# Two-layer hybrid backbone step: the last split weights of one token group used first for the other, the first modulation turned as one tile, grouped heads' scores in F32

## The chip, the cores and the metric

The kernel runs on one core of a Trainium2 chip. The metric is the device time of one execution in microseconds, as the median of several runs; less is better.

## The reference

One inference step of a two-layer backbone with model width 1024, for 128 context tokens and 512 latent tokens (640 in all). Each layer has a mixer and a SwiGLU FFN (hidden width 2816), each between an RMS norm with shift and scale before it and an RMS norm with a gate after it. Shift, scale and gate come from a small product, `silu(c) @ ada_w + ada_b`, one row for context and one for latent tokens. Layer 0 mixes with a short gated convolution and a conformer branch with a 31-tap depthwise convolution; layer 1 with grouped-query attention (8 heads of 64, 2 key heads) beside latent attention (8 heads); latent tokens read 640 keys, 128 cached and their own 512, context tokens their own 128. Cut to the parts that matter:

```python
hp = _modulate(_rmsnorm(xp, norm_pre[l, 0]), mp[:, 0], mp[:, 1])    # context; the same for latent (hs)
op = _conv_mixers(hp, *cargs)                                       # layer 0
q = _rmsnorm((h @ w_in)[..., :512].reshape(.., 8, 64), q_norm)      # layer 1, grouped heads
k = _rmsnorm((h @ w_in)[..., 512:640].reshape(.., 2, 64), k_norm)   # rotary on q and k of latent tokens
p = softmax(scale * q @ k.T); o = p @ v                             # context reads its 128 keys, latent 640: 128 cached and 512 own
xp = xp + mp[:, 2][:, None, :] * _rmsnorm(op, norm_post[l, 0])
fp = _modulate(_rmsnorm(xp, norm_pre[l, 1]), mp[:, 3], mp[:, 4])
xp = xp + mp[:, 5][:, None, :] * _rmsnorm(_swiglu(fp, w_gate, w_up, w_down), norm_post[l, 1])
```

All of it is in F32; the outputs are the tokens and the new key and value rows of the context.

## The kernel before

Activations lie with features on the 128 partitions and tokens along the free axis. A linear layer is split into two numbers of reduced precision (fp32r): `gran` (L123) loads a raw tile of 128x1024 weights through SP's queue, ACT casts it to `whi` (L134), VectorE (DVE) or GpSimd subtracts to give `wlo` (L139); `block` (L160) gives such pairs for some K tiles, and `mm3` (called by `lin`) issues three matmuls for each K tile, `whi` times the high half of x, `whi` times its low half, `wlo` times the high half (L175, L187, L189). `raw`, `whi` and `wlo` have four buffers each.

Tokens are worked on in groups: `GA` is columns 0 to 255, `GB` 256 to 639, `AB` both, `FULL` two of 320. A layer's stages overlap at their boundaries: where a mixer ends and the next stage begins, GA's boundary work (norms, gate, modulation) runs beside GB's products, and so GA goes first through the next stage's first blocks, then GB. In those places (`gu` and the last `down` of the FFN, `conv_in`'s first half, conv's and attention's output products, attention's input products) every weight block is loaded, cast and subtracted once for GA and once again for GB. Each boundary has statistics on PE (`st`), an inverse square root of twelve short DVE operations (`rvb`, `rgb`, `rhb`, then three rounds of `rtb`, `rtb`, `rzb`; L283 to L294), and `spread`, which hands the result to all partitions through PE. A scheduler puts the instructions of each engine in order at build time from its own estimates and from priorities; the engines then run in that fixed order.

The modulation: `ada0` at the start and, in the background of the convolution, `adaw` (a coroutine, `ada`, advanced by `spawn`) multiply c against `ada_w`, four column tiles of 2 rows (PE tile 128*2) into rows 0, 32, 64, 96 of one PSUM tile; `ada_out` copies four rows of two and turns them with sixteen tiny transposes (`adat`) into columns (`mods`). The depthwise convolution of the latent tokens is done on PE with 32*32 tiles (`tap`), 16 beside each other. The scores of a unit (one head, 128 queries) go into a PSUM tile `s` of two halves of 320 keys, of which there are two; then follow max, exponent, transposes (`pT`) on PE with copies to SBUF, and the value product (`av`) of two heads in column tiles of 64. The grouped heads' queries and keys are kept as high and low halves stacked on the partitions (`qS`, `kS`, `kL`, fp32r), the latent heads' as plain F32 (`qM`, `kM`).

The input projections of attention: for each group `attn_q` (products `pq`), `attn_kv` (`pkf`, `pvf`), `attn_k`, `attn_qa` (`pqa`, then `qa`), `attn_c` (`pcf`, `pkrf`), and `store_k`, `store_v`, `store_c`, which put keys, values and the compressed keys where attention reads them.

## Time and profile before

| | |
|---|---|
| median of three runs | 1697.18 us (1695.88 to 1697.71) |
| the profiled execution | 1697.65 us, span 1695.9 us |
| TensorE (PE) busy | 1632.8 us, 96% |
| weight loads of TensorE (PEld) | 1507.8 us, 89% |
| VectorE (DVE) | 968.0 us, 57% |
| ScalarE (ACT) | 655.1 us, 39% |
| GpSimd (POOL) | 217.3 us, 13% |
| read from memory | 190.99 MB, 116 GB/s over the span |

The table is from the profile's page of that execution. PE's share of the span does not say that it ran at its peak; the stages differ, which is why the profile is read by stage: start and first projection to 164 us, taps to 187, the rest of conv to 335, the FFN of layer 0 to 816, attention's projections to 945, attention to 1143, its output product to 1240, the FFN of layer 1 to the end. A row of the timeline gives start and length of merged instructions; because matmuls are pipelined, the time one of them costs is the distance from its start to the next start, not its length.

### The profile page before, as it was taken

How to read it: one execution, taken by the hardware profiler on the slowest of the kernel's cores; microseconds unless marked ns; L12 is line 12 of the kernel's file. 1: busy time of each engine (PE TensorE's matmuls, PEld its weight loads, DVE VectorE, ACT ScalarE, POOL GpSimd, SP SyncE). 2: the span in 40 equal slices, each digit the busy share in tenths (PEclk: the TensorE clock that was granted, in tenths of full speed). 3: DMA queues.
4: the chain of work that ended last, by engine and by line, in shares of the span. 5: the costliest groups of instructions: out<-in, count | busy, mean ns of one | idle time of the engine just before them, and what ended most of it. 6: DMA issues, size and time to landing. Idle time of an engine off the chain costs nothing.

```text
span 1695.9 us, 28690 instructions
## 1 busy us (share of the span) xinstructions
PE 1632.8 (96%) x11569; PEld 1507.8 (89%) x11569; DVE 968.0 (57%) x2021; ACT 655.1 (39%) x1222; POOL 217.3 (13%) x239
## 2 busy tenths in 40 slices
PE   6999999989999999999988899999999999999998
PEld 2577599989999999999988786769899999999998
DVE  3767055888784735837988655455888102111246
ACT  2321135653222211234555576665643222212234
POOL 2000000110000000001202121111102333333301
PEclk9999999999999999999999799999999999999999
DMA  9764014347463433525344010025354222222232
GB/s 339 233 222 148 30 50 130 113 129 226 143 200 112 137 100 98 157 88 174 104 136 100 8 38 14 1 80 173 119 174 151 78 85 75 75 76 75 75 108 104
DMA packets 174406, 198.37 MB, mean 117 GB/s; under 512 B 18788, under 2 KB 152881, under 8 KB 174273
## 3 DMA queue, kind: packets, MB, share of 16 engines
q1 hardware_dynamic: 172224, 194.94, 36.8%
q8 instruction: 90, 1.47, 0.4%
q10 hardware_dynamic: 1600, 1.49, 0.3%
q14 instruction: 44, 0.35, 0.1%
q0 software_dynamic: 448, 0.11, 0.0%
HBM read 190.99 MB, written 5.52 MB: 116 GB/s over the span
## 4 chain that ended last, share of the span: by engine, by line
PE 86%; DVE 8%; DMA 3%; issue 2%; ACT 1%; DVEq 0%; POOL 0%; SPq 0%; ACTq 0%; POOLq 0%
PE pd L175 6%; PE pd L187 6%; PE pd L189 6%; PE pu L175 6%; PE pu L189 6%; PE pu L187 6%; PE pg L189 5%; PE pg L175 5%; PE pg L187 5%; PE av L1408 3%; PE tap L787 2%; PE s L1355 2%; PE po L187 2%; PE po L175 2%; PE po L189 2%; PE pT L975 2%
## 5 line engine op out<-in xcount | busy, mean ns | idle before, releaser
L134 ACT CAST whi<-raw 128x1024 fp32r<-128x1024 f32 (+1 forms) x260 | 264.1, 1018 | 445.1 <-PE pd L187 112.1
L139 DVE TENSOR_TENSOR wlo<-raw,whi 128x1024 fp32r<-128x1024 f32 (+3 forms) x219 | 258.5, 1182 | 137.7 <-ACT whi L134 133.3
L175 PE MATMUL pd<-hid,whi 128*128 128x320 f32 (+2 forms) x704 | 181.5, 310 | 0.0
L189 PE MATMUL pd<-hid,wlo 128*128 128x320 f32 (+2 forms) x704 | 181.4, 309 | 0.0
L187 PE MATMUL pd<-hid,whi 128*128 128x320 f32 (+2 forms) x704 | 181.2, 309 | 0.0
L623 DVE TENSOR_TENSOR sg<-pu,sg 128x320 f32<-128x320 f32 (+2 forms) x88 | 39.9, 483 | 247.0 <-PE pu L189 247.0
L175 PE MATMUL pu<-h,whi 128*128 128x320 f32 (+2 forms) x704 | 177.0, 311 | 0.0
L187 PE MATMUL pu<-h,whi 128*128 128x320 f32 (+2 forms) x704 | 176.7, 310 | 0.0
L187 PE MATMUL pg<-h,whi 128*128 128x320 f32 (+2 forms) x704 | 176.6, 310 | 0.0
L189 PE MATMUL pg<-h,wlo 128*128 128x320 f32 (+2 forms) x704 | 176.2, 310 | 0.0
L189 PE MATMUL pu<-h,wlo 128*128 128x320 f32 (+2 forms) x704 | 176.1, 310 | 0.0
L175 PE MATMUL pg<-h,whi 128*128 128x320 f32 (+2 forms) x704 | 176.1, 310 | 0.0
L139 POOL TENSOR_TENSOR wlo<-raw,whi 128x1024 fp32r<-128x1024 f32 (+1 forms) x48 | 112.0, 2339 | 234.7 <-ACT whi L134 234.7
L385 DVE SCALAR_TENSOR_TENSOR acc<-adaw,cT,acc 128x512 f32<-128x512 f32 x168 | 123.9, 790 | 11.2 <-DMA adaw<-in_ada_w 11.0
L187 PEld LDWEIGHTS pd<-hid,whi 128*128 128x128 f32 x704 | 123.5, 188 | 0.0
L189 PEld LDWEIGHTS pd<-hid,wlo 128*128 128x128 f32 x704 | 123.5, 188 | 0.0
L175 PEld LDWEIGHTS pd<-hid,whi 128*128 128x128 f32 x704 | 123.4, 188 | 0.0
L187 PEld LDWEIGHTS pu<-h,whi 128*128 128x128 f32 x704 | 122.9, 189 | 0.0
L175 PEld LDWEIGHTS pu<-h,whi 128*128 128x128 f32 x704 | 122.8, 189 | 0.0
L189 PEld LDWEIGHTS pg<-h,wlo 128*128 128x128 f32 x704 | 122.7, 189 | 0.0
L187 PEld LDWEIGHTS pg<-h,whi 128*128 128x128 f32 x704 | 122.7, 189 | 0.0
L189 PEld LDWEIGHTS pu<-h,wlo 128*128 128x128 f32 x704 | 122.7, 189 | 0.0
(457 smaller groups left out, 3065.3 us busy)
## 6 DMA issues: line engine op xcount, KB each, us to landing
raw<-in_ffn_w_gate SPq DMA_DIRECT2D x56, 512.0 KB, 3.9
raw<-in_ffn_w_up SPq DMA_DIRECT2D x56, 512.0 KB, 3.7
raw<-in_ffn_w_down SPq DMA_DIRECT2D x56, 512.0 KB, 3.4
adaw<-in_ada_w SPq DMA_DIRECT2D x96, 256.0 KB, 3.0
raw<-in_ada_w SPq DMA_DIRECT2D x36, 512.0 KB, 4.1
raw<-in_conv_w_in SPq DMA_DIRECT2D x24, 512.0 KB, 4.5
raw<-in_attn_w_in SPq DMA_DIRECT2D x16, 512.0 KB, 4.1
raw<-in_attn_w_out SPq DMA_DIRECT2D x16, 512.0 KB, 3.5
```

The costliest lines, as they stand in the source:

```text
L134: nc.scalar.copy(hi[:, :kt, :cols], rv)
L139: (self.nc.vector if (le or next(self.lo_mix)) == "dve" else self.nc.gpsimd).tensor_tensor(o, x, h, ALU.subtract)
L175: ins = [mm(o, whi, h, start=first, stop=False) for o, (h, l) in zip(outs, xs)]
L187: mm(o, whi, l, start=False, stop=False)
L189: mm(o, wlo, h, start=False, stop=last)
L385: ins = nc.vector.scalar_tensor_tensor(acc[v], w, self.cT[:, v, k:k + 1], acc[v], ALU.mult, ALU.add)
L623: nc.vector.tensor_tensor(tv(sg[i]), uv, tv(sg[i]), ALU.mult)
L787: nc.tensor.matmul(ps[i][32 * j:32 * j + 32, :LAT], d[r, j], zs[j][r, at + t:at + t + LAT], start=(t == 0), stop=(t == CFK - 1))
L975: self.nc.tensor.transpose(ps, src, self.ident[:m, :m])
L1355: mm(o, qM[(h - 8) // 2][:96, h % 2, qs], kM[h - 8][:96, k0:k0 + n], start=True, stop=True)
L1408: nc.tensor.matmul(av[o:o + 64, :w], value(u.h, k), u.pt[:, 0] if qt == 0 else u.pt[:, :, i], start=(i == 0), stop=(i == len(ks) - 1))
```

## The change

Four edits. **Kept weights**: in each GA, GB pair the last blocks of GA (`gu` b = 2; `down`, conv out and attention out cb = 2, 3; both blocks of conv_in's first half; both of `attn_c`) are kept in their buffers and used first for GB, in the order 2, 3, 0, 1. **`ada_out`**: the PSUM tile is zeroed first, 98 rows are copied at once and turned with four transposes of 128x98, two additions of 16 columns follow; at the start this and the first modulation of GA have high priority. The coroutine `ada` starts at the first block of GB, before it started ahead of GA. **Scores of the grouped heads**: the query lies in F32 in `qF`, once plain and once with its halves exchanged, the keys in `kF` with keys 0 to 447 in rows 0 to 63 and 320 to 767 in rows 64 to 127 (from 448), and each half of the score block is one F32 matmul, from rows 0 to 63 and from rows 64 to 127 (a 64*128 tile). **Order of attention's projections**: `attn_c` of GB goes ahead of `attn_kv`, and the two `store_c` ahead of `attn_qa`.

```diff
+                nc.vector.memset(ps[:98], 0.0)
...
-        for j in range(4):
-            r = slice(32 * j, 32 * j + 2)
-            self.copy(engines[j], row[r], ps[r, :])
-        for j in range(4):
-            r = slice(32 * j, 32 * j + 2)
-            pt = alloc("adat")
-            for c in range(4):
-                self.nc.tensor.transpose(pt[:, 2 * c:2 * c + 2], row[r, c * P:(c + 1) * P], self.ident[r, r])
-            c0 = 4 * (ch + j)
-            for v in range(2):
-                self.nc.vector.tensor_tensor(self.mods[l][:, v, c0:c0 + 4], pt[:, :8].rearrange("p (c v) -> p v c", v=2)[:, v],
-                                             self.par["ada_b"][:, 48 * l + c0:48 * l + c0 + 4], ALU.add)
+        n = 512 // len(engines)
+        for i, e in enumerate(engines):
+            self.copy(e, row[:98, i * n:i * n + n], ps[:98, i * n:i * n + n])
+        pt = alloc("adat")
+        for c in range(4):
+            self.nc.tensor.transpose(pt[:, c * P:c * P + 98], row[:98, c * P:(c + 1) * P], self.ident[:98, :98])
+        o = pt.rearrange("p (c j r) -> p j c r", c=4, r=32)
+        c0 = 4 * ch
+        for v in (0, 1):
+            m, b = self.mods[l][:, v, c0:c0 + 16], self.par["ada_b"][:, 48 * l + c0:48 * l + c0 + 16]
+            q = lambda x: x.rearrange("p (j c) -> p j c", c=4)
+            self.nc.vector.tensor_tensor(q(m), o[:, :, :, v], q(b), ALU.add)
...
-        def gu(b, chunks):
-            g, u = self.block(wg, 0, KD, b * 256, 256), self.block(wu, 0, KD, b * 256, 256)
+        def gu(b, chunks, gu_=None):
+            g, u = gu_ or (self.block(wg, 0, KD, b * 256, 256), self.block(wu, 0, KD, b * 256, 256))
...
+        gu(2, ins[1], kept)
+        for b in range(2):
             gu(b, ins[1])
...
+                kept = {}
                 for ch in order:
-                    for cb in range(4):
-                        down(k0, kt, ch, cb, False)
+                    for cb in (range(4) if ch == order[0] else (2, 3, 0, 1)):
+                        w = down(k0, kt, ch, cb, False, kept.get(cb))
+                        if cb > 1:
+                            kept[cb] = w
...
+        with self.tc.high_priority(BOUND_PRIO):
+            self.ada_out(0, 0, ps, ("act", "dve"), self.pp)
+            for v in range(2):
+                nc.vector.scalar_tensor_tensor(a[:, v], m[:, v, KD:2 * KD], 1.0, self.par["norm_pre"][:, 0:KD], ALU.add, ALU.mult)
         H = [self.t5([P, 2, TOK], R32, name=f"h{k}") for k in range(KD)]
-        for v in range(2):
...
-        self.spawn(ada)
...
-            b2 = self.block(w, 0, KD, 3 * SCW + 512 + 256 * hb, 256)
-            b1 = self.block(w, 0, KD, 3 * SCW + 256 * hb, 256)
+            if (hb, chs) == (0, GB):
+                self.spawn(ada)
+            if chs != GB:
+                b2 = self.block(w, 0, KD, 3 * SCW + 512 + 256 * hb, 256)
+                b1 = self.block(w, 0, KD, 3 * SCW + 256 * hb, 256)
...
-                qS = st["qS"][t][:, hh, s:s + n]
-                nc.scalar.copy(qS[r], f[r])
-                nc.vector.tensor_tensor(qS[o], f[r], fl(qS[r]), ALU.subtract)
+                nc.scalar.copy(sw[o], f[r])
...
+    def keys_in(self, st, g, k0, x):
+
+        m = x.shape[1]
+        for a, b, r, c in ((k0, min(k0 + m, KH), 0, 0), (max(k0, KH), k0 + m, 64, KH - SEQ)):
+            if a < b:
+                self.copy(("act", "dve")[g], st["kF"][g][r:r + 64, a - c:b - c], x[:, a - k0:b - k0])
...
-            if ORD:
-                self.attn_c(H, GB, rb)
-                self.store_c(GA, st, ra)
-                self.store_c(GB, st, rb)
-                self.attn_qa(H, GB, st)
-            else:
-                self.attn_qa(H, GB, st)
-                self.store_c(GA, st, ra)
-                self.attn_c(H, GB, rb)
-                self.store_c(GB, st, rb)
+            self.store_c(GA, st, ra)
+            self.store_c(GB, st, rb)
+            self.attn_qa(H, GB, st)
...
-                    q, g = st["qS"][h // 2][:, h % 2, qs], h // 4
-                    mm(o, q, st["kS"][g][:, k0:k0 + n], start=True, stop=False)
-                    mm(o, q, st["kL"][g][:, k0:k0 + n], start=False, stop=True)
+                    r = slice(64 * c, 64 * c + 64)
+                    k0 = 0 if qt == 0 else SEQ
+                    mm(o, st["qF"][h // 2][r, (h + c) % 2, qs], st["kF"][h // 4][r, k0:k0 + n], start=True, stop=True)
```

What the new order looks like: names with numbers are buffers; `tap` is one tap of the convolution in one of sixteen tiles, `adaw` a matmul of the next modulation. On PE, in the last third of the taps, before (the rows of the second modulation are turned here):

```order
L787 MATMUL tap<-z_466,dg 32x512
L787 MATMUL tap<-z_467,dg 32x512
L470 MATMUL adat<-con,arow 128x2 x4
L787 MATMUL tap<-z_468,dg 32x512
L470 MATMUL adat<-con,arow 128x2 x4
L787 MATMUL tap<-z_465,dg 32x512
L787 MATMUL tap<-z_466,dg 32x512
```

and after, where the same modulation's matmuls now stand in three places among the taps, this one the second:

```order
L799 MATMUL tap<-z_445,dg 32x512
L456 MATMUL adaw<-raw,cM 2x512
L799 MATMUL tap<-z_446,dg 32x512
L799 MATMUL tap<-z_443,dg 32x512
L456 MATMUL adaw<-raw,cM 2x512
L799 MATMUL tap<-z_444,dg 32x512
L456 MATMUL adaw<-raw,cM 2x512
L799 MATMUL tap<-z_445,dg 32x512
L456 MATMUL adaw<-raw,cM 2x512
L799 MATMUL tap<-z_446,dg 32x512
L799 MATMUL tap<-z_443,dg 32x512
```

The turning left the taps and the products came into them. On PE at the end of attention's projections, where `pqa` is the last product, `rz` the inverse square roots that `spread` needs, `nc`, `stc` and `stqa` statistics and transposes of compressed keys and queries, before:

```order
L189 MATMUL pqa<-h_7893,wlo 128x384
L1352 MATMUL s<-kS_9087,qS_8345 128x128
L1353 MATMUL s<-kL_9089,qS_8345 128x128
L1352 MATMUL s<-kS_9087,qS_8345 128x128
L1353 MATMUL s<-kL_9089,qS_8345 128x128
L313 MATMUL spread<-con,rz 128x128 x2
L975 MATMUL nc<-con,cf0a 128x128
L975 MATMUL nc<-con,cf1a 128x128
L306 MATMUL stc<-con,csq 128x1 x3
L313 MATMUL spread<-con,rz 128x128 x3
L306 MATMUL stqa<-con,qsq 128x1 x3
L175 MATMUL mqr<-qa_8342,whi 128x320
```

and after:

```order
L190 MATMUL pqa<-h_7747,wlo 128x384
L1360 MATMUL s<-kF_8905,qF_8175 128x128 x2
L1360 MATMUL s<-kF_8905,qF_8175 128x320 x2
L997 MATMUL pT<-con,prob 128x128
L1360 MATMUL s<-kF_8905,qF_8175 128x320 x2
L997 MATMUL pT<-con,prob 128x128
L314 MATMUL spread<-con,rz 128x128 x2
L1360 MATMUL s<-kF_8905,qF_8175 128x320 x2
L997 MATMUL pT<-con,prob 128x128 x5
L997 MATMUL nc<-con,cf0a 128x128
L997 MATMUL nc<-con,cf1a 128x128
L307 MATMUL stc<-con,csq 128x1 x3
```

Four score blocks of head 0 and transposes of its first units now stand between the last product and the statistics. On DVE, in the boundary of the FFN before attention's projections, in the chain of twelve operations that ends in `rzb`, before (from its fourth operation):

```order
L291 TENSOR_TENSOR rtb<-rgb 128x3
L1044 TENSOR_TENSOR qS_8345<-qf,qS_8345 64x256 x2
L985 STREAM_SHUFFLE sw<-qf 128x128
L292 TENSOR_TENSOR rtb<-rtb,rhb 128x3
L139 TENSOR_TENSOR wlo<-raw,whi 128x1024
L987 TENSOR_TENSOR qf<-qf,rope 128x128
L294 SCALAR_TENSOR_TENSOR rzb<-rtb,rgb 128x3
L1044 TENSOR_TENSOR qS_8346<-qf,qS_8346 64x256
L1038 COPY ssq<-stq 128x2x2
L1044 TENSOR_TENSOR qS_8346<-qf,qS_8346 64x256
L139 TENSOR_TENSOR wlo<-raw,whi 128x1024
```

and after, from its first:

```order
L284 TENSOR_SCALAR rvb<-st 128x3
L286 TENSOR_SCALAR rgb<-rvb 128x3
L289 TENSOR_SCALAR rhb<-rvb 128x3
L292 TENSOR_TENSOR rtb<-rgb 128x3
L293 TENSOR_TENSOR rtb<-rtb,rhb 128x3
L295 SCALAR_TENSOR_TENSOR rzb<-rtb,rgb 128x3
L292 TENSOR_TENSOR rtb<-rzb 128x3
L293 TENSOR_TENSOR rtb<-rtb,rhb 128x3
L295 SCALAR_TENSOR_TENSOR rzb<-rtb,rzb 128x3
L292 TENSOR_TENSOR rtb<-rzb 128x3
L293 TENSOR_TENSOR rtb<-rtb,rhb 128x3
L295 SCALAR_TENSOR_TENSOR rzb<-rtb,rzb 128x3
```

The subtractions for the queries are gone, and neither weights nor rotary operations stand within the chain.

## Rows read from the trace of the kernel before

**Rows 1.** From the first part of the page: busy time, share of the span and instructions of each engine.
```profile
PE 1632.8 (96%) x11569; PEld 1507.8 (89%) x11569; DVE 968.0 (57%) x2021; ACT 655.1 (39%) x1222; POOL 217.3 (13%) x239
```

**Rows 2.** The table by stage: busy time of each engine in a stretch (with its instructions), TensorE's granted clock as a share of full speed, the share of the DMA engines and GB/s. The four stretches are the input projections of attention in three parts and the first part of attention.
```profile
816.50:868.70 52.20, 44.12 (x339) 42.76 (x337) 46.69 (x137) 26.53 (x48) 8.79 (x10) 0.93 0.50 150
868.70:926.60 57.90, 56.88 (x343) 54.45 (x344) 52.33 (x140) 29.49 (x67) 10.50 (x9) 1.00 0.34 83
926.60:945.00 18.40, 8.09 (x34) 7.14 (x33) 13.80 (x58) 7.39 (x17) 0.76 (x2) 0.58 0.25 57
945.00:1035.50 90.50, 88.27 (x611) 72.00 (x610) 55.09 (x105) 64.53 (x159) 18.91 (x43) 0.97 0.06 18
```

**Rows 3.** From the costliest groups on the page: line, engine, operation, output and inputs, count, then busy time and mean ns of one, then idle time before and who ended it.
```profile
L139 DVE TENSOR_TENSOR wlo<-raw,whi 128x1024 fp32r<-128x1024 f32 (+3 forms) x219 | 258.5, 1182 | 137.7 <-ACT whi L134 133.3
```

**Rows 4.** The waits of PE over the whole span: who waited for whom, us in total, times, longest.
```profile
PE st L519 <- DVE sq L516: 10.9, 6, 4.4
...
PE po L175 <- ACT z L268: 1.9, 1, 1.9
```

**Rows 5.** The timeline of PE in the depthwise convolution (taps), instructions of one kind in a row merged: start, us from first start to last end, line, operation, tile of the array (rows*columns), shape, count of records.
```profile
164.21 23.68 PE L787 MATMUL tap<-z,dg 32*32 32x512 f32 x724
187.82 1.02 PE L454 MATMUL adaw<-raw,cM 128*2 128x512 f32 x2
188.77 1.04 PE L787 MATMUL tap<-z,dg 32*32 32x512 f32 x2
189.74 1.02 PE L454 MATMUL adaw<-raw,cM 128*2 128x512 f32 x2
...
196.37 0.41 PE L470 MATMUL adat<-con,arow 2*128 2x2 f32 x4
```

**Rows 6.** From PE's groups by form: the scores of a latent head against one half of the keys.
```profile
L1355 PE MATMUL s<-kM,qM 96*128 96x320 f32 x128 | 41.5, 446 | 0.2 <-ACT prob L1383 0.2
```

**Rows 7.** The timeline of all engines at the start, around the first modulation.
```profile
33.84 1.03 PE L710 MATMUL ada<-ada0w,cM 128*2 128x512 f32 x4 [0.33 <-DMA ada0w<-in_ada_w]
...
41.86 1.87 PE L454 MATMUL adaw<-raw,cM 128*2 128x512 f32 x4 [2.37 <-DMA raw<-in_ada_w]
42.66 2.15 DVE L506 SCALAR_TENSOR_TENSOR u<-x,a,spread 128x128 f32<-128x128 f32 x8
...
44.64 1.87 PE L454 MATMUL adaw<-raw,cM 128*2 128x512 f32 x4 [0.91 <-DMA raw<-in_ada_w]
```

**Rows 8.** The waits of PE in the projections, from 816.5 to 945.
```profile
PE nk L975 <- DVE kfa L1088: 1.6, 1, 1.6
PE stk L1081 <- ACT sqk L1078: 1.6, 1, 1.6
PE spread L313 <- DVE rzb L294: 1.5, 1, 1.5
PE pcf L189 <- DVE wlo L139: 1.3, 1, 1.3
PE pcf L175 <- ACT cf0a L1070: 1.0, 1, 1.0
PE pcf L175 <- ACT whi L134: 0.8, 1, 0.8
```

**Rows 9.** DVE's groups by form from 816 to 945.
```profile
L1044 DVE TENSOR_TENSOR qS<-qf,qS 64x384 fp32r<-64x384 f32 x8 | 5.1, 633 | 0.3
...
L1044 DVE TENSOR_TENSOR qS<-qf,qS 64x256 fp32r<-64x256 f32 x8 | 3.6, 455 | 0.2
L139 DVE TENSOR_TENSOR wlo<-raw,whi 128x640 fp32r<-128x640 f32 x4 | 3.3, 820 | 0.0
```

**Rows 10.** The timeline of DVE, first and last operation of the chain that makes an inverse square root for a boundary.
```profile
827.16 0.16 DVE L283 TENSOR_SCALAR rvb<-st 128x3 f32<-128x3 f32 x1
...
837.63 0.15 DVE L294 SCALAR_TENSOR_TENSOR rzb<-rtb,rzb 128x3 f32<-128x3 f32 x1
```

**Rows 11.** The timeline of PE at the end of the projections; in brackets the idle time before and what ended it.
```profile
930.46 0.47 PE L1352 MATMUL s<-kS,qS 128*128 128x128 f32 x1 [3.57 <-ACT qaf L261]
...
934.75 1.22 PE L313 MATMUL spread<-con,rz 128*128 128x128 f32 x4 [3.61 <-DVE rz L294]
...
940.79 1.62 PE L313 MATMUL spread<-con,rz 128*128 128x128 f32 x6 [2.31 <-DVE rz L294]
```

**Rows 12.** The timeline of PE, two of the four matmuls of one score block of the grouped heads.
```profile
954.52 0.31 PE L1352 MATMUL s<-kS,qS 128*128 128x320 f32 x1
954.67 0.31 PE L1353 MATMUL s<-kL,qS 128*128 128x320 f32 x1
```

**Rows 13.** The timeline of PE around a value product (`av`), and the next transposes.
```profile
1057.80 0.71 PE L975 MATMUL pT<-con,prob 128*128 128x128 f32 x5
1058.43 2.38 PE L1408 MATMUL av<-pt,Vm 128*64 128x256 f32 x20
1060.74 0.49 PE L1355 MATMUL s<-kM,qM 96*128 96x128 f32 x2
1061.07 0.38 PE L975 MATMUL pT<-con,prob 128*128 128x128 f32 x2
```

**Rows 14.** The timeline of PE, five transposes and the four records of a latent head's score block.
```profile
1039.33 0.71 PE L975 MATMUL pT<-con,prob 128*128 128x128 f32 x5
1039.88 1.24 PE L1355 MATMUL s<-kM,qM 96*128 96x320 f32 x4
```

83 lines of the change are left out of this document (40 added, 43 removed).

## The prediction

> **What bounds the kernel now.** I read the first part of the page, then the table by stage, then the waits of TensorE (PE) in the stages that the change touches, and last single stretches. PE is busy 96% of the span, VectorE (DVE) 57% [rows 1], so a microsecond off DVE or ScalarE (ACT) is worth something only where PE waits for it. The table by stage [rows 2] says where that is: the attention stage has 2.2 us of gaps in 90.5; but from 816.5 to 945, the input projections of attention, PE is idle 8.1, 1.0 and 10.3 us, and the last of the three stretches runs at a granted clock of 0.58. The weight split itself (a cast on ACT, then a subtraction of 1.18 us on DVE for each tile [rows 3]) is hidden nearly everywhere: the waits for `whi` and `wlo` come to 0.8 and 1.3 us, both in the projections [rows 8]. All sums are made against the profiled execution, 1697.65 us, 0.5 above the median of 1697.18; its span is 1695.9 and 1.8 us lie around it. About 0.2% (3.4 us) is what a measurement here tells from no change.
>
> **Kept weights.** In each pair of token groups two of the weight blocks are no longer loaded, cast and subtracted a second time: 32 loads, as many casts and subtractions. In the FFN the cover is the matmuls of the block that is still there, and no wait for a weight stands there now, so I price it at nothing. All four `whi`/`wlo` buffers are full while the kept block is used twice, so the next split can begin only when the first half of the block is free; the other half's 48 products, at 0.15 us from start to start [rows 12], are then 7.2 us of cover for two casts and two subtractions, and the raw weights, in buffers of their own, are there by then. What it can give is at boundaries, where DVE and ACT have the split and the next operand to make: the conv output product waits 1.9 us for `z` [rows 4], with splits queued on the same two engines. I take that away and 3.1 more from the like places at out_proj and the FFN's ends (10.9 us of waits for `sq` in all [rows 4], most of them in groups whose loads don't change): **-5**, from 0 to -8.
>
> **The modulation row (`ada_out`).** Four rows of transposes become one; each row's four tiny transposes take PE 0.40 us (196.37 [rows 5]). In conv eight such groups become two, of a full array: six times 0.40, and one tap piece that stood alone between two of them, some 0.95 as between two `adaw` (below) instead of 0.07: -3.3; I say **-2.6**, since the new ones are larger.
> At the start the chain copies, transposes, additions, scale, first `u` runs from the end of the last `ada` matmul at 34.9 to 42.7 [rows 7]; with one transposed tile and high priority it should be 5 us shorter. But DVE still has four weight subtractions of some 1.2 us in that stretch and eight modulations to make, and the first block's weights are among the four. Between -5 (the chain alone decides) and +2 (the modulation, put first, now delays the weights); I take **-2**, nearer to DVE's sum.
>
> **The moved modulation of the next layer (`adaw`).** It now starts one block later. On PE a row of two `adaw` matmuls that sits among taps or projections takes 0.95 us, and one alone takes the same 0.95 [rows 5]: two column tiles run beside each other, one alone wastes the slot. By the instruction order the slots go from 34 (24 pairs, 4 singles, one row of four, one of eight) to 41 (23 pairs, 18 singles), and two of the 34 ran while PE had nothing else (41.86 and 44.64 [rows 7]), which those of after can't: 9 x 0.95 = +8.5. Three of the places are brackets among the taps, where there was one. In a run, taps cost 23.61 us for 724 records (164.21 to 187.82), 0.033 each, since 16 tiles of 32x32 run together; a piece of two or four records between two `adaw` costs 0.96 [rows 5]. Pieces go from 3 to 9: 6 x (0.96 - 0.09) = +5.2. Its loads (0.5 MB each on SP, through the four raw buffers) now queue in the second group, which has no weights to load, and then beside the weights of the later products, where PE waits for none today. Together **+13.7**, from +10 (two more of them fall into idle time) to +15.
>
> **Grouped heads' scores.** Before, a block of two 320-key halves is four single-pass matmuls, 0.15 us from start to start [rows 12], 0.59 in all. After, it is one F32 matmul for each half, 64 rows deep, the halves in different rows of the array. An F32 matmul of 320 columns is two records; four of them, the two halves of a latent head, take 1.24 us from first start to last end, one 0.446 by itself, so (1.24 - 0.446) / 3 = 0.27 a record [rows 6, 14]. Nowhere does this trace show a pair of 64-row tiles. The nearest rows are the taps, where four row groups, each with its own PSUM tile, and four column groups run together [rows 5], and the value product, two column tiles of 64: its 20 records of 256 columns take 2.31 us (1058.43 to 1060.74 [rows 13]), 0.115 each, where one in turn would be 0.27 x 256/320 = 0.21. I take it that the halves run side by side: two slots, 0.54, against 0.59: 32 blocks x -0.05 = -1.6. The other end is one after the other, 1.08: 32 x 0.49 = +15.6.
> But the tile shape changes. From `pT` at 1057.80 to `pT` at 1061.07 go 3.27 us, of which five transposes are 0.55 (1039.33 to 1039.88 [rows 14]), ten slots of 0.21 are 2.1 and two 96-row records of 128 columns some 0.24; about 0.35 is left for going into column tiles and out again, 0.175 a change [rows 13]. Among the taps a lone `adaw`, two records of 512 columns, which are 0.86 by the 0.27, takes 0.95 (187.82 to 188.77): 0.09 a change [rows 5]. In the instruction order of the attention part the changes go from 98 to 150. 52 changes are 4.7 by the one and 9.1 by the other; I take the middle, 6.8, since a pair of halves lies between these shapes. So **+5.2** for both, from -1.6 (row tiles change for nothing) to +7.5, with the halves together.
> The Trainium skill ("TensorEngine Tiling (Array Packing)", Tiling Modes, Key Properties) says that changing the tiling mode drains TensorE, and makes no exception for row tiles. By that the 52 changes cost what those of the value product do, and the sum would be 2.3 higher; the trace agrees for column tiles (0.35 for in and out), and for row halves no run here shows it.
>
> **The projections.** The high halves of the queries and keys, and their low ones, go: DVE loses eight `qS` subtractions of 0.633 and eight of 0.455, the key's (some 6 us with their casts) and, with the kept block, four subtractions of weights at 0.82 [rows 9]: 8.7 + 6 + 3.3 = 18 us, of 112.8 busy in the three stretches [rows 2], and gets about 1 us of copies. Where it counts: (a) the chain `rvb` to `rzb`, twelve short operations, stands from 827.16 to 837.78, with `qS`, `wlo` and rotary operations queued between them [rows 10]; after, the order has the twelve in a row (2.4 us at 0.2), and the normalised tokens of the second group come sooner. PE's waits there, `sqk` 1.6, `rzb` 1.5, `whi` 0.8, `wlo` 1.3, `cf0a` 1.0, `kfa` 1.6 [rows 8], are 7.8: I take 5. (b) At the end, 926.6 to 945, PE stands still three times, 3.6 before `s`, 3.6 and 2.3 before `spread` [rows 11], 10 us with the small ones. `attn_c` of the second group moves to the front: with its block kept it issues no load and nothing on SP, only its products and three copies on ACT, and what then stands behind it on PE, the keys' product, is not what anyone waits for. `attn_qa` comes last, and four units of scores and transposes, some 5 us of PE work that is due anyway, stand between the spreads. I take 7, and 2 for the clock, of 8.1 us that ran at 0.58 [rows 2]. What is late next is `spread` behind `rz`, since the chain itself stays. Together **-14**, from -5 to -22.
>
> **The sum.** -2 (start) - 5 (kept weights) - 2.6 (`ada_out`) + 13.7 (`adaw`) + 5.2 (scores) - 14 (projections) = -4.7, from 1697.65: **1693**.
>
> **Rivals.**
> *The halves run one after the other.* Everything as above, but a score block takes four slots: +17 on the sum (15.6 and the 1.6 not gained), **1710**. For it: no 64-row pair is in the trace, and F32 makes two records of each matmul, which one queue could hand on in order. Against: taps show exactly this, two records each and 16 tiles together [rows 5]. It decides from the point at which an isolated block starts its next operation over 0.8 us after its first. The Trainium skill (same page, Restrictions and Gotchas, PSUM Pressure) says that different row tiles cannot use one PSUM bank at the same time; the halves write `s[:, 0]` and `s[:, 1]`, 512 numbers apart, so by that rule they don't meet. Taps, which give every row group a PSUM tile of its own, agree.
> *DVE's relief doesn't become PE time.* The projections are bound by the chain of statistics, from token to `spread` to `h`, and by the order in which PE meets them, not by DVE's sum: it is 89% busy in the first stretch and 90% in the second, but 75% in the last, where PE waits most [rows 2]. Then the projections give 5 instead of 14, the waits move to other tiles: +9, **1702**, slower than before. It decides if PE's idle time from 816 to the first full attention unit stays above 14 us of now 19.4.
> *The gaps close altogether.* The projections give 22 instead of 14 and the start 5 instead of 2, and the changes cost 0.09: -8 - 3 - 2.1 on the sum, **1680**.
>
> **How the numbers follow.** Forecast 0.55, halves in turn 0.10, relief lost 0.20, gaps closed 0.15. The forecast, 1693 with 5 us to either side from its own bounds, is 0.25% below the median, so its weight divides 0.32 faster, 0.18 same, 0.05 slower. Relief lost lies on the edge: 0.07 same, 0.13 slower. Faster 0.32 + 0.15 = 0.47, same 0.25, slower 0.05 + 0.13 + 0.10 = 0.28. The range takes in relief lost and most of the closed gaps and leaves the halves in turn out: 1681 to 1705.
>
> **What would show it.** Right: taps take about 10 us more, with three brackets of `adaw` instead of one; a 320-key block of the grouped heads shows its four records as two pairs, each pair starting together, and 0.15 to 0.2 us more to its neighbours than its records need; PE's idle time from 816 to the end of the projections falls from 19 to under 9, with score records between the spreads; FFN stages stay within 1 us. Wrong: waits for `whi` or `wlo` in the second groups (the kept buffers), the start's first `ub` not earlier than 44, or four record starts one after the other in a score block.

## The result and the profile after

The changed kernel takes 1708.86 us (median of 4 runs, 1706.82 to 1710.71) beside 1696.53 for the kernel before (1695.26 to 1697.71): ratio 1.0074, with a 95% interval of 1.0062 to 1.0086. It is 12 us slower, outside the range and on the other side of the forecast. The profiled execution took 1706.82 us with a span of 1704.9, so the traces hold 9.0 of the 12 us.

The first row of the page after, busy time of each engine:

```profile
PE 1646.3 (97%) x11533; PEld 1497.1 (88%) x11533; DVE 919.8 (54%) x1938; ACT 617.8 (36%) x1180; POOL 215.9 (13%) x239
```

Against [rows 1] VectorE lost 48 us, ScalarE 37, and 16 MB less are read (175.13 of 190.99); PE is 13.5 us busier. So the work that was to go has gone, off the path; what came is on PE. Where, the two traces show by the distance between the first PE records of each stage (in us, worked out from the rows of each trace; the last column is the span):

```
        to ub  to tap   taps  to po  to pg   FFN0  attention part  out    FFN1   tail    span
before  46.44  117.77  45.53  63.02  62.42  481.35      326.82    62.59  478.78  11.16  1695.9
after   38.36  116.37  53.61  69.03  60.60  485.75      320.97    62.59  482.75  14.93  1704.9
forecast: 9.1 more up to po, 5 less at the boundaries, 8.8 less in the attention part
measured: 4.6 more up to po, 10.3 more in "to pg", both FFNs and the tail, 5.9 less in attention
```

`ub` is the first conv projection, `po` conv's output product, `pg` the first FFN product; the attention part runs from the first `pq` to the last `rsum`; the tail begins at the first `xT`, the turning of the outputs. Two terms are off by 3 to 4.5 us; the kept weights, whose term is the one at the boundaries, are off by 15. A sign of being right failed with them: the FFN stages were to stay within 1 us, and they are 4.4 and 4.0 longer.

PE's waits, after:

```profile
PE st L521 <- DVE sq L518: 20.7, 7, 5.0
PE s L1360 <- ACT prob L1390: 9.0, 5, 7.2
...
PE po L176 <- ACT z L269: 1.9, 1, 1.9
```

The wait for `z`, which I took away, stands as it did, and the wait for `sq` has doubled [rows 4]. The longest, on PE at the start of the first FFN, and DVE beside it:

```profile
342.15 0.28 PE L190 MATMUL pg<-h,wlo 128*128 128x256 f32 x1
347.41 1.23 PE L521 MATMUL st<-con,sq 128*128 128x1 f32 x6 [4.98 <-DVE sq L518]
348.50 0.56 PE L176 MATMUL pg<-h,whi 128*128 128x256 f32 x1
348.86 0.41 PE L188 MATMUL pg<-h,whi 128*128 128x256 f32 x1
349.07 0.41 PE L190 MATMUL pg<-h,wlo 128*128 128x256 f32 x1
```
```profile
340.39 0.55 DVE L518 TENSOR_TENSOR sq<-sq 128x384 f32<-128x384 f32 x1
340.86 2.35 DVE L140 TENSOR_TENSOR wlo<-raw,whi 128x1024 fp32r<-128x1024 f32 x2
343.13 0.55 DVE L518 TENSOR_TENSOR sq<-sq 128x384 f32<-128x384 f32 x1
343.60 1.21 DVE L140 TENSOR_TENSOR wlo<-raw,whi 128x1024 fp32r<-128x1024 f32 x1
344.73 2.53 DVE L518 TENSOR_TENSOR sq<-sq 128x384 f32<-128x384 f32 x4
```

`sq` is the running sum of squares over the eight feature tiles of GB, in the order 0 to 7. PE is out of products at 342.4, and DVE has five of the seven additions still to make, with weight subtractions among them. The order 2, 3, 0, 1 of the blocks hands over feature tiles 4 to 7 first and 0 to 3 last, and the sum begins at tile 0: nothing can be added until the third block of four is done. The wait costs twice, as the stretches behind it show (busy time of PE, PEld, DVE, ACT and POOL, granted clock, DMA share, GB/s):

```profile
347.00:352.00 5.00, 4.59 (x22) 4.62 (x23) 2.08 (x13) 0.77 (x1) 0.00 (x0) 0.56 0.26 93
352.00:357.00 5.00, 5.00 (x35) 5.00 (x34) 4.70 (x8) 1.61 (x4) 2.87 (x3) 0.76 0.37 105
357.00:363.00 6.00, 6.00 (x52) 6.00 (x52) 6.00 (x10) 4.04 (x7) 3.68 (x4) 1.00 0.01 3
```

Products that stood 0.12 us apart ahead of the wait (342.03 to 342.15) stand 0.21 apart behind it (348.86 to 349.07).

### The profile page after: what moved, and what is told of

The parts are those of the page before. It is cut to its first block, busy times and chain, and to the rows that moved or that the text cites. A ratio compares the mean times of both kernels' runs of the same rounds, so it can differ in the third digit from the quotient of the medians.

```text
span 1704.9 us, 28360 instructions
## 1 busy us (share of the span) xinstructions
PE 1646.3 (97%) x11533; PEld 1497.1 (88%) x11533; DVE 919.8 (54%) x1938; ACT 617.8 (36%) x1180; POOL 215.9 (13%) x239
## 3 DMA queue, kind: packets, MB, share of 16 engines
HBM read 175.13 MB, written 5.52 MB: 106 GB/s over the span
## 4 chain that ended last, share of the span: by engine, by line
PE 88%; DVE 5%; DMA 3%; ACT 2%; issue 1%; POOL 0%; SPq 0%; DVEq 0%; POOLq 0%; ACTq 0%
PE pd L176 6%; PE pd L188 6%; PE pd L190 6%; PE pu L176 6%; PE pu L188 6%; PE pu L190 6%; PE pg L176 6%; PE pg L188 6%; PE pg L190 6%; PE av L1415 3%; PE tap L799 2%; PE adaw L456 2%; PE po L188 2%; PE po L176 2%; PE po L190 2%; PE pT L997 2%
## 5 line engine op out<-in xcount | busy, mean ns | idle before, releaser
L135 ACT CAST whi<-raw 128x1024 fp32r<-128x1024 f32 (+1 forms) x228 | 232.5, 1021 | 493.5 <-PE pd L188 115.7
L140 DVE TENSOR_TENSOR wlo<-raw,whi 128x1024 fp32r<-128x1024 f32 (+2 forms) x187 | 221.6, 1186 | 179.3 <-ACT whi L135 165.2
L188 PEld LDWEIGHTS pg<-h,whi 128*128 128x128 f32 x704 | 124.0, 191 | 0.0
L176 PEld LDWEIGHTS pg<-h,whi 128*128 128x128 f32 x704 | 123.9, 191 | 0.0
L188 PEld LDWEIGHTS pd<-hid,whi 128*128 128x128 f32 x704 | 123.4, 188 | 0.0
```

What stands on the lines that cost most here:

```text
L135: nc.scalar.copy(hi[:, :kt, :cols], rv)
L140: (self.nc.vector if (le or next(self.lo_mix)) == "dve" else self.nc.gpsimd).tensor_tensor(o, x, h, ALU.subtract)
L176: ins = [mm(o, whi, h, start=first, stop=False) for o, (h, l) in zip(outs, xs)]
L188: mm(o, whi, l, start=False, stop=False)
```

## The experiments

Ratios are to the kernel before, of runs on the same chip, with 95% intervals. Differences between two changed kernels are of medians; by the ratios, for which the kernel before was timed anew each time, they come out up to 1.6 us larger or smaller. None of the kernels leaves out a part of the computation. Each diff is cut to the lines that matter.

**The order of the sum alone.** The changed kernel, with the squares of the second group, and of the last norm, added in the order in which their products come:

```diff
-        for k in range(KD):
-            q = self.addsq(st, ys[k], k, n, q, (b, 0))
+        for i, k in enumerate((4, 5, 6, 7, 0, 1, 2, 3) if chunk == GB and H is not None else range(KD)):
+            q = self.addsq(st, ys[k], k, n, q, (b, 0), last=i == KD - 1)
```

> The changed kernel, but the sums of squares at the boundary of the second group (and in the last norm) take the features in the order in which the products now deliver them, 4 to 7 and then 0 to 3. Theory A (the loss sits in the boundaries: the sum starts at feature 0, which the new block order delivers in the second half, so seven of eight additions wait for the last products and TensorE stands before the statistics, 5.0, 3.5, 3.8 and 3.3 us, with the clock halved behind the long ones): the statistic waits fall back to what they were before the change, 12 to 16 us less, 1693 to 1697. Theory B (the kept blocks hold all four weight buffers, so the splits behind them are late, and the sums are late because of that): nothing changes, 1706 to 1711.

1700.04 us, 1.0013 [1.0001, 1.0025]: 8.8 us of the loss (10 by the ratios) are gone by one loop's order. The tail is 11.52 again, FFN0 481.49, FFN1 478.52, and the wait for `sq` is below that of before [rows 4]:

```profile
PE st L521 <- DVE sq L518: 8.4, 5, 2.6
```

**No weights kept**, everything else as changed:

```diff
-            for cb in (range(4) if ch == GA else (2, 3, 0, 1)):
+            for cb in range(4):
...
-                wt = kept[cb] if cb in kept else self.block(w, 0, KD, cb * 256, 256)
+                wt = self.block(w, 0, KD, cb * 256, 256)
```

> The changed kernel with the kept weights undone: every block is loaded and split again for the second group, in the order 0 to 3; the rest as changed. Theory A and theory B both: the statistic waits go back to 10 to 12 us in all, 1694 to 1700. Against e1 it sizes what keeping the weights gives by itself: by my prediction 5 us in boundaries and some 3 in the projections, so e1 5 to 8 us faster than e2; if the subtractions were hidden all along, e1 and e2 are within 3 us of each other.

1699.0 us, 1.001 [1.0001, 1.0019]. Within 1 us of the reordered sum, with intervals that overlap: the 32 loads, casts and subtractions that keeping saves (VectorE is busy 952.3 us here and 918.7 there) are worth nothing that shows, and the cost of the edit was the order that came with it.

**The scores as before**, everything else as changed:

```diff
-                    mm(o, st["qF"][h // 2][r, (h + c) % 2, qs], st["kF"][h // 4][r, k0:k0 + n], start=True, stop=True)
+                    mm(o, q, st["kS"][g][:, k0:k0 + n], start=True, stop=False)
+                    mm(o, q, st["kL"][g][:, k0:k0 + n], start=False, stop=True)
```

> The changed kernel with the grouped heads' scores as before (halves in reduced precision, four matmuls a block, their copies and subtractions on VectorE); the rest as changed. If the F32 scores cost what I predicted on TensorE (5 us) and VectorE's relief gives 5 to 10 in the projections: 1709 to 1714. Rival (the changes of tile shape are dearer than the relief is worth): 1700 to 1705.

1714.68 us, 1.0102 [1.0087, 1.0117]: 5.8 slower than with F32 scores. In the changed kernel they are no part of the loss.

**The next modulation early**, as before the change:

```diff
-            if (hb, chs) == (0, GB):
-                self.spawn(ada)
...
+        self.spawn(ada)
         made = set()
```

> The changed kernel with the next modulation started ahead of the first group again, as before the change; the rest as changed. The instruction order then has one bracket of single matmuls among the taps instead of three. Theory: the brackets cost 8 to 10 us and the early place 4 to 5 in the first block, so 4 to 6 us faster, 1702 to 1705. Rival (the start's gain of some 8 us came from taking the modulation out of the first block): 1708 to 1714.

1700.41 us, 1.0019 [1.001, 1.0029]: the later start costs 8.5 us. The taps are 41.02 us long instead of 53.61 (one bracket of `adaw` instead of three), conv's rest 63.02 instead of 69.03, and the first projection 10.7 longer, where the early products stand.

**Both repairs**, the sum's order and the early modulation:

```diff
+        self.spawn(ada)
         made = set()
...
+        for i, k in enumerate((4, 5, 6, 7, 0, 1, 2, 3) if chunk == GB and H is not None else range(KD)):
```

> The changed kernel with both repairs: sums of squares in the order of delivery and the next modulation started early. If the two losses stand apart, the gains add: 1708.9 - 8.8 - 8.5 = 1691.6, faster than before the change by 5. If the early modulation and the boundaries share the same idle time, less: 1695 to 1698.

1691.55 us, 0.9971 [0.9959, 0.9982]. The two costs add up, by the medians: 8.8 and 8.5 alone, 17.3 together.

**No weights kept, and the modulation early**:

```diff
-        gu(2, ins[1], kept)
-        for b in range(2):
+        for b in range(3):
             gu(b, ins[1])
...
+        self.spawn(ada)
         made = set()
```

> The changed kernel without kept weights and with the modulation started early, so that the F32 scores, the one-tile turning and the new order of the projections are left: 1708.9 - 9.9 - 8.5 = 1690.5 if the effects add. If keeping the weights is worth anything once its boundary order is repaired, this is slower than the kernel with both repairs, by my prediction 5 to 8 us; if the split was hidden all along, the two are within 2 us.

1690.05 us, 0.9964 [0.9951, 0.9977]: again no worse than with kept weights.

**F32 scores alone** on the kernel before:

```diff
-                    mm(o, q, st["kS"][g][:, k0:k0 + n], start=True, stop=False)
-                    mm(o, q, st["kL"][g][:, k0:k0 + n], start=False, stop=True)
+                    mm(o, st["qF"][h // 2][r, (h + c) % 2, qs], st["kF"][h // 4][r, k0:k0 + n], start=True, stop=True)
```

> The kernel before with the F32 scores alone (queries and keys in F32, one matmul for each half from different row halves), the order of the projections as before. If the 5.8 us that undoing them cost is their own: 1691. If the gain needs the new order of the projections (score units between the spreads): 1696 to 1700, the price of the shape changes showing. If TensorE's row halves cost what I took, the attention stage itself is 5 us longer and the projections 10 shorter.

1691.99 us, 0.9976 [0.9966, 0.9985].

**The turning as one tile with the start's priority**, alone on the kernel before:

```diff
-                self.nc.tensor.transpose(pt[:, 2 * c:2 * c + 2], row[r, c * P:(c + 1) * P], self.ident[r, r])
+            self.nc.tensor.transpose(pt[:, c * P:c * P + 98], row[:98, c * P:(c + 1) * P], self.ident[:98, :98])
...
+        with self.tc.high_priority(BOUND_PRIO):
+            self.ada_out(0, 0, ps, ("act", "dve"), self.pp)
```

> The kernel before with the one-tile turning and the start's priority alone. My prediction took -2 for the start and -2.6 for the turning: 1692.5. Rival, from the run with the modulation started early, whose taps began 2 us later than before the change although its first projection began 8 us earlier: the first block is bound by its weights, nothing is won, 1696 to 1699.

1686.13 us (1683.74 to 1689.62), 0.9941 [0.9926, 0.9956]: the lowest median of all versions, ahead of both kernels. In its trace the way to the first tap is 162.22 us instead of 164.21, the taps 41.02 instead of 45.53, and, with no edit there, the attention part 320.8 instead of 326.8.

**Turning, priority and F32 scores** on the kernel before:

```diff
+            self.ada_out(0, 0, ps, ("act", "dve"), self.pp)
...
+                    mm(o, st["qF"][h // 2][r, (h + c) % 2, qs], st["kF"][h // 4][r, k0:k0 + n], start=True, stop=True)
```

> The kernel before with the one-tile turning, the start's priority and the F32 scores, but the old order of attention's projections, the modulation early and no kept weights. It differs from the run without kept weights and with the modulation early (1690.0) by the order of the projections alone. Theory: the new order puts score blocks ahead of the statistics, whose exponent waits for the queries' inverse square root, 6.7 us in one wait, so the old order is faster and the gains of start and scores add: 1682 to 1684. Rival: both kernels with one edit won the same 5.5 us in the projections by where the scheduler put the score blocks, so it counts once: 1686 to 1690.

1688.31 us, 0.9951 [0.9938, 0.9965]: 2.2 above the turning with priority, by intervals that overlap: no gain on top of it. The gains of the two in the attention part, 6.0 and 5.5, are the same microseconds.

**The new order of attention's projections alone** on the kernel before:

```diff
+            self.attn_c(H, GB, rb)
             self.attn_kv(H, GB, rb)
...
+            self.store_c(GA, st, ra)
+            self.store_c(GB, st, rb)
+            self.attn_qa(H, GB, st)
```

> The kernel before with the new order of attention's projections alone (compressed keys of the second group ahead, loaded again; both stores of compressed keys ahead of the latent queries). Theory: it costs by itself, through score blocks that stand before their scale is there, 1700 to 1704. Rival: no effect by itself, 1695 to 1698. My prediction took it for a gain of some 7 us: 1690.

1696.31 us, 1.0001 [0.9992, 1.0009]: nothing.

**Both repairs with the old order of the projections**:

```diff
+            self.attn_qa(H, GB, st)
             self.store_c(GA, st, ra)
+            self.attn_c(H, GB, rb)
             self.store_c(GB, st, rb)
-            self.attn_qa(H, GB, st)
```

> The kernel with both repairs (sums in the order of delivery, modulation early; 1691.6) with the old order of attention's projections, so that only attn_c's blocks aren't kept. If the new order costs 5 to 8 us: 1684 to 1687, and within 2 us of the kernel with start and scores alone, since keeping the weights gave nothing; if not: 1690 to 1693.

1690.36 us, 0.9965 [0.9952, 0.9977], beside 0.9971 with the new order: no difference that the intervals tell.

The last three ask where the gain of the turning comes from, its 6 us of the attention part first. **Two score blocks behind the first `spread`** in the kernel before, by a dependence of order only, on the first of their matmuls:

```diff
+                    ins = mm(o, q, st["kS"][g][:, k0:k0 + n], start=True, stop=False)
+                    if self.mark is not None:
+                        self.tc.add_manual_dep(ins.ins, self.mark.ins.name, mybir.DependencyInfo(
+                            mybir.DependencyClass.NoSync, mybir.DependencyReason.DATA), reason="order")
```

> The kernel before, with one thing moved: the first two score blocks (128 keys) and their maxima stand behind the first spread of the compressed keys' norm instead of ahead of it; every other row of every engine's order stays where it was. The kernel with start and turning alone stands so, and its projections and attention are 6.0 us shorter than before in the profile without any edit there. Theory A (the score blocks ahead of the spread are what cost those 6 us): 1690 to 1691.5. Theory B (the first spread waits for an inverse square root that stands on VectorE behind splits, copies and squares, 8.2 us after the last product before the change and 3.8 there, and VectorE is busy throughout, so only the two maxima of 0.28 us leave its way): 1694.5 to 1696.

1696.51 us, 1.0 [0.9991, 1.0009]: no change. With the scores out of the way `spread` still comes 7.6 us behind the last product; it waits for its own `rz`:

```profile
925.72 0.34 PE L189 MATMUL pqa<-h,wlo 128*128 128x384 f32 x1
933.32 1.20 PE L313 MATMUL spread<-con,rz 128*128 128x128 f32 x4 [7.26 <-DVE rz L294]
```

**That root first on DVE**, in the kernel before, ahead of the two `kM` copies, a `qsq`, a low half of `qa` and two maxima, by the same kind of dependence:

```diff
+        if s == 0:
+            self.mark = self.rs
...
+                    ins = nc.vector.tensor_copy(kM[2 * t + hh][64:96], st["krt"])
+                    if t == 0:
+                        self.after_rs(ins)
```

> The kernel before, where on VectorE the last seven operations of the first compressed-key inverse square root (rt, rz) stand ahead of two key copies, one square sum, one low half and two maxima instead of among them; PE's order is the old one. Theory B (the end of the projections is bound by where this chain stands among other work on VectorE): the first spread comes 2.5 to 3.3 us earlier, and the kernel is 2 to 4 us faster, 1692.5 to 1694.5. Rival (the operations that now stand behind it are needed by the second spread and the latent queries, so the wait moves there): 1695.5 to 1697.

1695.72 us (1693.12 to 1701.23), 0.9998 [0.9989, 1.0006]. `spread` comes 5.3 us behind the last product (926.72 to 932.04) instead of 8.4, but the next step, `cf0a`, then stands behind what was pushed back:

```profile
932.04 1.22 PE L320 MATMUL spread<-con,rz 128*128 128x128 f32 x4 [1.21 <-DVE rz L301]
934.93 0.48 PE L982 MATMUL nc<-con,cf0a 128*128 128x128 f32 x1 [1.68 <-DVE cf0a L1155]
...
939.18 1.62 PE L320 MATMUL spread<-con,rz 128*128 128x128 f32 x6 [2.31 <-DVE rz L301]
```

**The turning without the priority**:

```diff
-        self.ada_out(0, 0, ps, ("act", "dve") * 2, self.pp)
+        self.ada_out(0, 0, ps, ("act", "dve"), self.pp)
```

> The kernel before with the one-tile turning alone, without the start's priority. It splits the 10 us of the kernel with both. By the stages of that profile the turning is worth 4.5 us among the taps and 1.5 in the rest of conv, the start 2, and 6 came in the projections with no edit there. If the turning is alone the cause of conv's part and the projections' gain came with any new schedule: 1688 to 1690. If the start's priority carries the projections' gain with it: 1692 to 1694.

1687.8 us, 0.9947 [0.9934, 0.996]: the intervals overlap those with priority; the first `ub` comes at 38.72 instead of 38.92. The turning is the edit that pays; the priority adds nothing that shows.

## Why the prediction was wrong, point by point

**Kept weights: the step that failed.** "No wait for a weight stands there now, so I price it at nothing", and -5 in the sum. The first half was right: leaving out the loads gives nothing, whichever way the rest stands (1700.04 beside 1699.0, 1691.55 beside 1690.05). The second half, what it gives at the boundaries, took the waits there, for `z` and `sq` [rows 4], to be about busy engines, and asked only what the edit takes off DVE and ACT. It did not ask in which order the products reach their consumer. In the order 2, 3, 0, 1 half the features are late for a sum that runs from 0 to 7. So the term that stood at -5 measured +9.9: undoing the keeping gives back 9.9 us, undoing the sum's order alone 8.8; that is shown. The wait for `z` did not go either.

**The later modulation: right mechanism, mis-sized.** Forecast +13.7; +8.5 by the medians, between the changed kernel and the one with the early start. The three brackets stand among the taps as forecast, each matmul alone at 0.95 and each tap piece between at 0.97 to 0.98, the second of them:

```profile
188.60 1.02 PE L456 MATMUL adaw<-raw,cM 128*2 128x512 f32 x2
189.55 1.05 PE L799 MATMUL tap<-z,dg 32*32 32x512 f32 x4
190.53 1.02 PE L456 MATMUL adaw<-raw,cM 128*2 128x512 f32 x2
191.48 1.04 PE L799 MATMUL tap<-z,dg 32*32 32x512 f32 x2
```

The taps' 12.6 us and conv's 6.0 behind them came, and 10.7 left the first projection. Charged by the distance to the next start, the tap records cost 6.2 us more than with the early start (42.2 and 36.0), where the sum had 5.2. The `adaw` records cost only 3.9 more (39.1 and 35.2), where it had 8.5 for their slots: it counted them from the kernel before, where `adaw` costs 32.9 and two of its rows ran while PE had nothing else. With the shorter start they have no such place in either kernel. Another 4.3 us come back as less idle time and cheaper `ub` records.

**The turning (`ada_out`): right, and the clock came on top.** The taps lost 4.5 us instead of 2.6 (45.53 to 41.02, in the kernel with turning and priority). But 3.0 of the 4.5 can come without any edit here: in the kernel with F32 scores alone, where the old turning stands among the taps in the same places, they take 42.56. The difference is TensorE's granted clock, which in the kernel before fell to its lower level in the last third of the taps, while PE was busy throughout, and did not fall there; a stretch before, then all the taps of the kernel with F32 scores alone (columns as above):

```profile
199.00:206.00 7.00, 7.00 (x136) 3.56 (x137) 0.58 (x6) 0.00 (x0) 0.00 (x0) 0.51 0.01 3
```
```profile
165.52:208.08 42.56, 41.83 (x1017) 22.79 (x1016) 5.57 (x19) 3.95 (x7) 0.20 (x4) 1.00 0.17 51
```

Of the five traces with the old turning, four have such a fall among the taps; of the eleven with the new one, none. What sets it off is not shown. Against the kernel with F32 scores alone, the new turning takes 2.6 us off the `adat` and `tap` records of the first projection and the taps together, the forecast's figure. The larger transposes are cheap; in the kernel with the early modulation the turning among the taps is one row:

```profile
196.56 1.90 PE L799 MATMUL tap<-z,dg 32*32 32x512 f32 x34
198.39 0.56 PE L470 MATMUL adat<-con,arow 98*128 98x98 f32 x4
198.87 1.74 PE L799 MATMUL tap<-z,dg 32*32 32x512 f32 x37
```

It takes 0.48 from its start to the next tap. A group of tiny ones took 0.33 so read, from 196.37 [rows 5] to the next row (the prediction's 0.40 is a length), and left a lone tap piece of 0.98:

```profile
196.70 1.04 PE L787 MATMUL tap<-z,dg 32*32 32x512 f32 x2
197.68 0.40 PE L470 MATMUL adat<-con,arow 2*128 2x2 f32 x4
```

**The start: the number right, the reason only in part.** -2 was forecast and 2.0 came (164.21 to 162.22, in the kernel with turning and priority). The chain is short now, as forecast, and a weight's cast is waited for next, after:

```profile
34.91 0.85 PE L470 MATMUL adat<-con,arow 98*128 98x98 f32 x4 [0.47 <-ACT arow L269]
...
36.28 2.16 DVE L508 SCALAR_TENSOR_TENSOR u<-x,a,spread 128x128 f32<-128x128 f32 x8
...
38.36 0.80 PE L176 MATMUL ub<-h,whi 128*128 128x256 f32 x2 [2.61 <-ACT h L509]
40.46 0.79 PE L176 MATMUL ub<-h,whi 128*128 128x256 f32 x2 [1.31 <-ACT whi L135]
```

The first `u` runs 6.4 us earlier than in [rows 7], the first `ub` 8.1. In the kernel with turning and priority the first `ub` comes 7.5 earlier, and the stretch from there to the taps is 5.5 longer. The wait for a weight, which is what the forecast counted on, is 1.3 of that. `adaw` costs 3.3 more there, with the two rows that ran in idle time before [rows 7]; `ub` costs 2.1 more, at a granted clock of 0.98 instead of 0.99; the new turning takes 1.1 off. That the sum of these comes out at the forecast's number is luck. Without the priority the first tap comes at 162.54, so the transposed tile does it.

**The halves of a score block: together, as forecast; the change of shape dearer.** After, PE between transposes:

```profile
966.13 0.71 PE L997 MATMUL pT<-con,prob 128*128 128x128 f32 x5
966.77 0.81 PE L1360 MATMUL s<-kF,qF 64*128 64x320 f32 x4
967.51 0.33 PE L997 MATMUL pT<-con,prob 128*128 128x128 f32 x1
967.77 1.51 PE L1415 MATMUL av<-pt,Vg 128*64 128x256 f32 x12
```

Four records take 0.74 from start to next start, where four in turn would be 1.08; in the trace the two of a pair start 6 to 7 ns apart. The rival with the halves in turn is out. What a pair costs once the shape is set shows where two blocks follow each other, in the kernel with turning, priority and F32 scores:

```profile
938.75 1.35 PE L1349 MATMUL s<-kF,qF 64*128 64x320 f32 x8
940.03 0.44 PE L1404 MATMUL av<-ptp,Vg 128*64 128x128 f32 x4
```

Eight records take 1.28, 0.54 more than four: 0.27 a pair, the slot of the sum. The rest is the change of shape. By medians over blocks among transposes the step from `pT` into the block is 0.20 us, the block 0.74 and the transpose behind it 0.17, 1.11 in all. Around a latent head's block of 96 rows, which is F32 too and runs among the same transposes, the first and the last of these steps are 0.11 and 0.11. So going in and out costs 1.11 - 0.54 - 0.22 = 0.35, as much as for the value product (0.35 [rows 13]), where I took 6.8 for 32 blocks, 0.21 each. The Trainium skill ("TensorEngine Tiling (Array Packing)", Tiling Modes, Key Properties) says that changing the mode drains TensorE; the 0.35 agrees for row halves too. The Trainium skill's rule on PSUM banks (same page, Restrictions and Gotchas, PSUM Pressure) agrees with halves in two banks running together; halves in one bank were not tried.

Before, the three steps were 0.03, 0.67 and 0.11, so a block among transposes is 0.30 dearer. Blocks that follow a value product pay 0.10, since the array changes shape there anyway. A ledger of PE's time in the attention part shows the whole price, 6.5 where the sum had 5.2: each record is charged the distance to the next start, less the idle time (worked out from the traces, us; score blocks are the grouped heads', "turning" is the kernel with its priority):

```
                                          before  after  scores alone  turning alone  both
score blocks, transposes, value products   112.7  119.2      118.4         112.2     120.4
PE idle                                     22.1   15.1       13.0          17.5      12.3
spread, statistics, first latent product    16.5   11.0       11.2          15.7      11.7
the other products                         175.3  175.4      178.4         175.1     176.9
```

So alone, F32 scores cost PE some 6 us in the first line and 3 in the last, and bring back 9 of idle time and 5 in the third line. On top of the turning they cost 8 and 2 and bring back 5 and 4: nothing is left, and the medians, 2.2 slower, don't tell it from no change. The value of that edit hangs on what else is waiting.

**The projections: mechanism right in part, size nearly.** Forecast -14; the ledger, over the whole attention part, has 7.0 of idle time less and 5.5 less in `spread`, the statistics and the first latent product, much of which ran at a granted clock of 0.58 before [rows 2]: 12.5 in all. The stages as in [rows 2], with bounds moved with the products (columns as above):

```profile
823.70:870.20 46.50, 42.19 (x337) 41.62 (x336) 41.88 (x126) 24.66 (x49) 8.89 (x10) 0.93 0.52 156
870.20:928.20 58.00, 57.17 (x344) 54.54 (x345) 42.88 (x115) 30.08 (x65) 11.10 (x9) 1.00 0.31 80
928.20:946.30 18.10, 10.63 (x53) 6.29 (x54) 14.90 (x55) 11.18 (x28) 1.55 (x5) 0.72 0.26 58
```

PE is idle 12.6 us in them instead of 19.4, neither under 9, as the forecast had it, nor above 14, from which the rival with the lost relief decides. At the end the score records do stand between the statistics, but PE stops ahead of them:

```profile
928.05 0.71 PE L1360 MATMUL s<-kF,qF 64*128 64x128 f32 x4
935.93 1.44 PE L1360 MATMUL s<-kF,qF 64*128 64x320 f32 x4 [7.17 <-ACT prob L1390]
...
939.34 1.06 PE L314 MATMUL spread<-con,rz 128*128 128x128 f32 x4
...
945.74 0.91 PE L314 MATMUL spread<-con,rz 128*128 128x128 f32 x6 [0.21 <-DVE rz L295]
```

One wait of 7.2 stands for three of 3.6, 3.6 and 2.3 [rows 11]: the third block needs a score buffer, its owner the exponent, and that the maxima, which DVE makes at 934.42 and 935.08, behind subtractions and copies. The step that gave the new order 7 us was wrong: alone it is worth nothing (1696.31), with both repairs nothing that shows (1691.55 with it, 1690.36 without), and with the scores as before PE idles 14.0 us between the last product and the first `mqr`, where it idled 10.3 before.

**What stays open.** The turning alone shortens the attention part by 6 us without an edit there, and there the scheduler put DVE's work behind the last product in another order:

```profile
918.08 0.34 PE L189 MATMUL pqa<-h,wlo 128*128 128x384 f32 x1
921.88 1.20 PE L313 MATMUL spread<-con,rz 128*128 128x128 f32 x4 [3.47 <-DVE rz L294]
...
928.07 1.62 PE L313 MATMUL spread<-con,rz 128*128 128x128 f32 x6 [2.31 <-DVE rz L294]
```

`spread` comes 3.8 us behind the last product, 8.4 before. That this order is the cause is not shown. Neither the place of two score blocks nor that of the first root on DVE is by itself the whole of it, as two runs showed: in their traces the attention part is 324.6 and 324.0 us instead of 326.8, a part of the 6, and the stage behind it 1.6 longer at a granted clock of 0.97 instead of 1.00; their times don't differ from before.

## What to carry to other kernels

When an edit changes the order in which blocks are produced, ask first who consumes them and in which order: a running sum that starts at the late end costs more than all the loads saved. Work taken off engines that PE does not wait for is worth nothing, as the 34 us that keeping the weights took off VectorE, and two edits that fill the same gap count once. A small edit can come with another order of work or another granted clock in places far from it, worth 3 to 6 us here, so time each part alone before the whole: here one part of four, the turning, did as well as any version (1687.8 us alone, 1686.1 with the priority), and the whole lost 12.

## What the runs showed of the hardware

- Behind a wait of 5.0 us PE's granted clock was 0.56 for some 5 us and 0.76 for the next 5, and 1.00 only in the stretch from 10 us after the wait: the products in between took 0.21 us instead of 0.12.
- The granted clock fell to 0.51 for 7 us among 32*32 taps while PE was busy throughout, and cost 3.0 us; the same taps ran at 1.00 in another kernel, and what decides is not shown.
- Two F32 matmuls of 64 rows, in different halves of the array, run side by side: two of 320 columns take 0.54 us together, as one of 96 rows does. Going in and out among full-array transposes costs 0.35 more.
- One set of four 98x98 F32 transposes takes 0.48 us among 32*32 taps; a set of four 2x2 transposes takes 0.33.
